# Sharing out the PSUM banks of two attentions anew: two banks for scores, other banks for the outputs of the values

## The chip, the cores and the metric

The kernel runs on one core of a Trainium2 chip. The metric is the device time of one execution in microseconds (us). The core has a matrix engine, TensorE (PE in the profile), which multiplies and transposes, and writes its results into PSUM, a memory of eight banks of 128 partitions by 512 float32 values. VectorE (DVE), ScalarE (ACT) and GpSimd (POOL) do the elementwise work; SyncE (SP) issues the loads. Each engine works through its own list of instructions in order, and an instruction that needs another engine's result waits for a semaphore; whatever is queued behind it waits with it. A PSUM bank can take new results only when the old ones have been read, so a tile that gets a bank waits for the last reader of the tile that had it before.

## The reference

A sequence of 512 tokens with 1024 features goes through two layers, each an attention, an output projection, a layer norm, a SwiGLU FFN and a layer norm.

```
# layer A: differential attention, 8 heads, two score matrices (m) for each
for i in range(s // Q_BLOCK):                       # 4 query tiles of 128
    sc = einsum('bqhmd,bkhmd->bhmqk', q[:, q0:kend], k[:, :kend])
    p = softmax(where(allowed, sc, neg))
    a = p[:, :, 0] - lam * p[:, :, 1]
    outs.append(einsum('bhqk,bkhe->bqhe', a, v[:, :kend]))
o = rms_norm(concatenate(outs), subln_g) * (1.0 - lambda_init);  return o @ w_o
# layer B: band attention, 16 heads, learned bias, one shared K/V
sc = einsum('bnqhd,bnkhd->bhnqk', q, k_band) + bias
p = softmax(where(band_valid, sc, neg))
o = einsum('bhnqk,bnkhd->bnqhd', p, v_band);  return o @ w_o
# both
x = layer_norm(ALPHA * x + mix);  x = layer_norm(ALPHA * x + (silu(gate) * up) @ w_out)
```

All data is float32; the large products are made of three matrix products of parts rounded to a shorter format (`hi`/`lo` of the weights, `xTh`/`xTl` of the activations, `oTh`/`oTl` of the attention's outputs).

## The kernel before, in words

Each layer's attention is cut into 32 units: 8 heads (in layer B pairs of heads) times 4 query tiles; a unit of query tile `qt` has `(qt + 1) * 128` keys. The units run through a software pipeline written out by hand. A step of layer A's pipeline (`STEPS`, line 50) issues on TensorE: the scores `s` of unit i, filling work, the product with the values `o` of unit i-2, the transpose `ot` of unit i-3, more filling work, and the transposes `at` of unit i-1. The filling work is the q, k and v projections of later heads and, at the end, the first matmuls of the output projection. `weave` mixes the two by the rates in `FA` and `FB`, with a model of how long each engine takes; `chain` and `later` put the work of the other engines in their queues when the model says that its inputs are there. So the order of each engine's list follows from the model, and a tile's bank enters into it, because the model knows when the bank's last tile was read.

What one unit of layer A does (`unit_a`): `sc`, two score tiles (m = 0, 1) on TensorE; VectorE adds the mask and takes the row minimum of the negated sum (`masked`, the profile's `e<-sc,mask` and `nm`); ScalarE takes the exponentials with their sum; VectorE mixes the two (`e<-e,c`); TensorE transposes (`at`), ScalarE copies the result (`aT`), TensorE multiplies with the values (`o`); ScalarE squares it for the norm (`sq`), GpSimd makes the root (`ms`, `rr`), VectorE scales (`sq<-o,rr,gsub`); TensorE transposes again (`ot`), ScalarE rounds it into `oTh`, and VectorE takes the rest (`oTl<-ot,oTh`). The q and k projections end in a rotation, on VectorE in part: `krc`, `kla_g`, `ks`, `qs`.

In layer B (`unit_b`, `values_b`) a unit has the scores `sc_b` of two heads, `masked` with the bias, the exponentials, the scaling (`e_b<-e_b,r_b`), and the transposes `pt_b` of each head, which ScalarE (`pth`) and VectorE (`ptl<-pt_b,pth`) read; when a pair's four query tiles are there, `values_b` makes `po` for each of its heads, which ScalarE (`tl`) and VectorE (`ot<-po,tl`) read.

The banks: the pool `psp` has four tags of two banks. `pj` serves the projections. `sc0` and `sc1` serve the scores, one bank of each per unit (`pair`), so two units' scores fit. `sm` serves in layer A `at`, `o` and `ot`, in layer B `pt_b` and `po` of both heads. Within a tag the banks are given in turn. The output projection takes `pj` and a `pair` for the first half of its columns, two pairs for the second.

Of the kernel before, what the change touches and what calls it, by code (L numbers as in the profile page):

```python
# [132 lines left out]
def trunk(ctx, tc, x, a_w_qkv, a_lambda, a_subln_g, a_w_o, kv_w, b_w_q, b_rel_bias, b_w_o,  # L133
# [29 lines left out]
    def new(pool, bufs, shape, dtype, tag, name):  # L163

        old = slots.setdefault((pool.name, tag), [])
        if len(old) >= bufs:
            settle([old[-bufs]])
        t = pool.tile(shape, dtype, tag=tag, name=name)
        if len(old) >= bufs:
            model.replaces(name_of(t), old[-bufs])  # L170
        old.append(name_of(t))
        return t

    def bank(tag, name):
        return new(psp, 2, [P, HALF], F32, tag, name)

    def pair(name):
        return [bank(f"sc{i}", f"{name}_{i}") for i in range(2)]

    def passed(out_, ins, ns, start):  # L180
        at = max([clk[0]] + [model.ready(a) for a in ins] + ([model.unused(out_)] if start else []))
# [270 lines left out]
    def project_out(act, nk, get_xres, banks0, lead, held, gate, ln, tr, name, banks_1=None):  # L452

        begun = banks_1 is not None  # L460

        def step(h, b, t, k, w_, j):
            ts_ = slice(t * P, (t + 1) * P)
            ah, al = act(h, k)
            token_major(b, ah[:, ts_], al[:, ts_], w_[0][:, j, :], w_[1][:, j, :],
                        k == 0 and not begun, k == nk - 1)
            return True

        def add(h, t, b):
            residual(xres[t], b, h, sts[t])  # L470

        b01 = banks0(0)
        ws = []
        for c in range(lead // 2):
            while not gate(2 * c + 1):
                yield True
            ws.append(take(f"{name}_0_{c}"))
            for j in range(2):
                for t in range(2):
                    yield step(0, b01[t], t, 2 * c + j, ws[c], j)  # L480
        while not gate(-1):
            yield True
        b23 = banks0(1)
        for c in range(lead // 2):
            for j in range(2):
                for t in range(2):
                    yield step(0, b23[t], 2 + t, 2 * c + j, ws[c], j)
            free(f"{name}_0_{c}")
        xres = get_xres()
        for c in range(lead // 2, nk // 2):  # L490
            while not gate(2 * c + 1):
                yield True
            w_ = take(f"{name}_0_{c}")
            for j in range(2):
                for t in range(NT):
                    yield step(0, (b01 + b23)[t], t, 2 * c + j, w_, j)
            free(f"{name}_0_{c}")
        sts = []
        for t in range(NT):
            sts.append(small.tile([P, 2, 6], F32, tag="st", name=f"st_{name}_{t}"))  # L500
        for t in (2, 3, 0, 1) if lead else range(NT):
            add(0, t, (b01 + b23)[t])
        banks = banks_1 or pair(f"{name}_1a") + pair(f"{name}_1b")
        split = (nk - held) // 2
        for c in range(split):
            w_ = take(f"{name}_1_{c}")
            for j in range(2):
                for t in range(NT):
                    yield step(1, banks[t], t, 2 * c + j, w_, j)
            free(f"{name}_1_{c}")  # L510
        ws = []
        for t in range(NT):
            for i in range(held // 2):
                if t == 0:
                    ws.append(take(f"{name}_1_{split + i}"))
                for j in range(2):
                    yield step(1, banks[t], t, 2 * (split + i) + j, ws[i], j)
                if t == NT - 1:
                    free(f"{name}_1_{split + i}")
            add(1, t, banks[t])  # L520
            ln(t, xres[t], sts[t])
            if tr and t in (1, 2):
                tr(t - 1, xres[t - 1])
# [519 lines left out]
    def unit_a(h, qt):  # L1043

        kend = (qt + 1) * P
        n_ = f"{h}_{qt}"
        sc = pair(f"sc_{n_}")
        scores(sc, *qk[h], qt)
        e = new(ap3, 3, [P, 2, HALF], F32, "e", f"e_{n_}")
        nm = ap6.tile([P, 2], F32, tag="nm", name=f"nm_{n_}")  # L1050
        s = ap6.tile([P, 2], F32, tag="s", name=f"s_{n_}")
        r = ap6.tile([P, 2], F32, tag="r", name=f"r_{n_}")

        def top():
            masked(sc, (mask, mask), e, nm, kend)

        def ex():
            for m in range(2):
                act_e.activation(e[:, m, :kend], e[:, m, :kend], AF.Exp, scale=-1.0, bias=nm[:, m:m + 1],
                                     accum_out=s[:, m:m + 1])  # L1060

        def mix():
            vec_e.reciprocal(r, s)
            c = ap6.tile([P, 1], F32, tag="c", name=f"c_{n_}")
            vec_e.scalar_tensor_tensor(c, s[:, 0:1], r[:, 1:2], nlam, op0=ALU.mult, op1=ALU.mult)
            vec_e.scalar_tensor_tensor(e[:, 0, :kend], e[:, 1, :kend], c, e[:, 0, :kend],
                                           op0=ALU.mult, op1=ALU.add)

        chain([*sc, e], (lambda: sc, top), (lambda: [nm], ex), (lambda: [s], mix))
        yield e  # L1070
        pt = bank("sm", f"at_{n_}")
        for kt in range(qt + 1):
            transpose(pt[:, kt * P:(kt + 1) * P], e[:, 0, kt * P:(kt + 1) * P])
        aT = new(ap2, 2, [P, HALF], F32, "aT", f"aT_{n_}")
        chain([aT, pt], (lambda: [pt], lambda: act_e.copy(aT[:, :kend], pt[:, :kend])))
        yield aT
        po = bank("sm", f"o_{n_}")
        for kt in range(qt + 1):
            mm(po[:, 0:P], aT[:, kt * P:(kt + 1) * P], vt[kt][:, h * P:(h + 1) * P],
               start=(kt == 0), stop=(kt == qt), cost=4.0)  # L1080
        sq = new(ap2, 2, [P, P], F32, "sq", f"sq_{n_}")
        ms = ap6.tile([P, 1], F32, tag="ms", name=f"ms_{n_}")
        rr = ap6.tile([P, 1], F32, tag="rr", name=f"rr_{n_}")

        def root():
            pool_e.tensor_scalar(ms, ms, 1.0 / P, SUBLN_EPS, op0=ALU.mult, op1=ALU.add)
            pool_e.tensor_tensor(rr, ms, mexp, op=ALU.pow)
            pool_e.tensor_tensor(rr, rr, r[:, 0:1], op=ALU.mult)

        chain([sq, po], (lambda: [po], lambda: act_e.activation(  # L1090
            sq, po[:, 0:P], AF.Square, scale=r[:, 0:1], accum_out=ms)), (lambda: [ms], root), (
            lambda: [rr], lambda: vec_e.scalar_tensor_tensor(sq, po[:, 0:P], rr, gsub, op0=ALU.mult, op1=ALU.mult)))
        yield sq
        pu = bank("sm", f"ot_{n_}")
        transpose(pu[:, 0:P], sq)
        oh = oTh[:, h, qt * P:(qt + 1) * P]
        chain([pu, oTh, oTl], (lambda: [pu[:, 0:P]], lambda: act_e.copy(oh, pu[:, 0:P])), (
            lambda: [oh], lambda: vec_e.tensor_sub(
                oTl[:, h, qt * P:(qt + 1) * P], pu[:, 0:P], oh.bitcast(F32))))
        yield  # L1100
# [38 lines left out]
    def o_proj(oh, ol, res_src, l, name):  # L1139
        def get_xres():  # L1140
            del xres[:]
            for t in range(NT):
                xt = resid.tile([P, D], F32, tag="res", name=f"{name}_x_{t}")
                load_e.dma_start(xt, res_src(t))
                xres.append(xt)
            lng.append(ln_params(l, 0))
            return xres

        def banks0(i):
            if i == 0:  # L1150
                return [bank("pj", f"{name}_0_{j}") for j in range(2)]
            return pair(f"{name}_0_23")

        def gate(k):
            return done["s"] if k < 0 else done["o"] >= k

        yield from project_out(
            lambda h, k: (oh[:, k, :], ol[:, k, :]), KT, get_xres, banks0, 6, 8, gate,
            lambda t, xr, st: spill(layer_norm(xr, st, *lng[-1], f"{l}0_{t}"), x1d[l], t, xr),
            lambda t, xr: transpose_split(xr, t), name)  # L1160
# [123 lines left out]
    def unit_b(p, qt):  # L1284
# [1 line left out]
        bias = biases[p]  # L1286
        kend = (qt + 1) * P
        n_ = f"b{p}_{qt}"
        sc = pair(f"sc_{n_}")
        scores(sc, *qk[p], qt)  # L1290
        e = new(bp2, 2, [P, 2, HALF], F32, "e", f"e_{n_}")
        mx = small.tile([P, 2], F32, tag="nm", name=f"mx_{n_}")
# [17 lines left out]
        yield e  # L1310
        _, pth, ptl = held[p]
        for m in range(2):
            pt = bank("sm", f"pt_{n_}_{m}")
            for kt in range(qt + 1):
                transpose(pt[:, kt * P:(kt + 1) * P], e[:, m, kt * P:(kt + 1) * P])
            dh = pth[m][:, qt * P:qt * P + P]
# [11 lines left out]
    def values_b(p):  # L1328
# [1 line left out]
        ot = new(bp2, 2, [P, S], F32, "ot", f"ot_{p}")  # L1330
        steps, used = [], [ot, oTh, oTl]
        for m in range(2):
            po = bank("sm", f"po_{p}_{m}")
            for kt, lo in ((0, 0), (1, 128), (2, 256), (3, 256)):
                for i, src in enumerate((pth[m], ptl[m])):
                    mm(po[:, lo:S], vs[:, kt, m, :, :].rearrange("p a e -> p (a e)"),
# [100 lines left out]
```

## Time and profile before

| | us |
|---|---|
| median of 3 runs | 1239.59 (1236.62 to 1242.48) |
| the profiled execution, own time | 1239.44 |
| its span | 1237.7 |
| PE busy in the span | 1192.2 (96%) |
| DVE busy | 834.9 (67%) |
| ACT busy | 556.3 (45%) |
| POOL busy | 405.5 (33%) |

The span reaches from the first to the last recorded instruction of the core; the own time of the execution has a little around it. "Busy" counts the time in which an engine computes. The attentions run from about 45 to 240 us (layer A) and from about 660 to 860 us (layer B), each with its projections and followed by output projection and FFN. An engine's wait is put down to the instruction that released it, with the line of that one.

### The profile page before, as it was taken

Reading aid. Unit: us, or ns where it says so; the run is one execution under the profiler, and the core shown is the slowest. Engines: PE = TensorE matmul, PEld = TensorE weight load, DVE = VectorE, ACT = ScalarE, POOL = GpSimd, SP = SyncE. Lnnn points to the kernel's source line nnn. Section 1 sums busy time; section 2 is a strip of 40 time slices with the busy share of each in tenths; the row PEclk is TensorE's granted clock in tenths of the full one; section 3 lists DMA queues with packets and bytes.
Section 4 is the critical chain, followed back from the end, with each engine's and each line's share of the span. In section 5 each row is a group of like instructions: output and inputs, shape, how many; then the busy total and the mean of one; then the engine's idle time right before and its main releaser. Section 6 shows DMA issues by size and latency. Waiting matters only on the chain.

```text
span 1237.7 us, 19979 instructions
## 1 busy us (share of the span) xinstructions
PE 1192.2 (96%) x7640; PEld 1078.5 (87%) x7640; DVE 834.9 (67%) x1451; ACT 556.3 (45%) x1049; POOL 405.5 (33%) x410
## 2 busy tenths in 40 slices
PE   8989989899999999999999999989999999999997
PEld 7867877788999999888887888978899999998886
DVE  4677777388678888533465767675888888883327
ACT  4556666425444444322145667663454444443220
POOL 1134343421555564000323233214136666620022
PEclk9999999899999999999999999999999999999999
DMA  8433342245544443533344342335433333353311
GB/s 265 124 89 95 87 110 86 76 153 145 153 139 138 138 124 104 187 98 124 102 119 116 98 120 65 107 94 170 135 98 108 103 103 103 103 176 114 102 68 69
DMA packets 164191, 145.74 MB, mean 118 GB/s; under 512 B 6096, under 2 KB 137456, under 8 KB 164096
## 3 DMA queue, kind: packets, MB, share of 16 engines
q1 hardware_dynamic: 164096, 144.47, 38.6%
q8 instruction: 60, 0.98, 0.3%
q14 instruction: 35, 0.29, 0.1%
HBM read 127.63 MB, written 13.67 MB: 114 GB/s over the span
## 4 chain that ended last, share of the span: by engine, by line
PE 86%; DVE 7%; ACT 3%; issue 2%; DMA 1%; POOL 1%; SPq 0%; DVEq 0%; ACTq 0%; POOLq 0%
PE m L194 31%; PE c L194 5%; PE a L194 5%; PE b L194 5%; PE gu L194 5%; PE d L194 4%; PE vb_ps L194 4%; PE bk_ps L194 3%; PE bq_ps L194 3%; PE va_ps L194 3%; PE q_ps L194 2%; PE k_ps L194 2%; PE sc_b L194 2%; PE po L194 2%; PE pt_b L199 2%
## 5 line engine op out<-in xcount | busy, mean ns | idle before, releaser
L75 ACT ACTIVATE sg<-sg 128x512 f32<-128x512 f32 x38 | 24.1, 633 | 194.8 <-DVE sg L75 194.8
L75 POOL TENSOR_TENSOR sums<-raw_u 128x512 f32<-128x512 f32 x38 | 49.0, 1291 | 190.6 <-DVE s3lo L75 173.3
L75 POOL TENSOR_TENSOR lo_fo<-raw_fo,hi_fo 128x1024 fp32r<-128x1024 f32 x8 | 19.2, 2394 | 217.2 <-ACT hi_fo L75 217.2
L75 DVE TENSOR_TENSOR lo_fk<-raw_fk,hi_fk 128x1024 fp32r<-128x1024 f32 x28 | 33.9, 1223 | 66.4 <-ACT hi_fk L75 66.4
L75 POOL TENSOR_TENSOR sums<-raw_g,sums 128x512 f32<-128x512 f32 x38 | 76.6, 2016 | 0.0
L75 DVE TENSOR_TENSOR m<-m,m 128x256 f32<-128x256 f32 x76 | 31.7, 417 | 62.8 <-PE m L194 62.8
L75 ACT CAST hi_fk<-raw_fk 128x1024 fp32r<-128x1024 f32 x28 | 29.4, 1052 | 76.0 <-PE d L194 70.9
L75 DVE TENSOR_TENSOR alo<-raw_g,ahi 128x1024 fp32r<-128x1024 f32 x38 | 55.0, 1447 | 0.0
L75 POOL TENSOR_TENSOR sums<-sums,raw_g 128x512 f32<-128x512 f32 x38 | 49.8, 1311 | 3.9 <-DMA raw_g<-in_ffn_w_in_dram 1.1
L75 POOL TENSOR_TENSOR sums<-raw_g,raw_u 128x512 f32<-128x512 f32 x38 | 50.1, 1319 | 0.0
L75 DVE TENSOR_TENSOR s1lo<-sums,s1hi 128x1024 fp32r<-128x1024 f32 x38 | 46.0, 1211 | 0.0
L75 DVE TENSOR_TENSOR s3lo<-sums,s3hi 128x1024 fp32r<-128x1024 f32 x38 | 46.0, 1211 | 0.0
L75 ACT CAST hi_fo<-raw_fo 128x1024 fp32r<-128x1024 f32 x16 | 16.9, 1055 | 64.5 <-PE d L194 64.5
L194 PE MATMUL m<-T1h,s1hi 128*128 128x256 f32 x152 | 43.0, 283 | 0.0
L194 PE MATMUL m<-T1l,s1hi 128*128 128x256 f32 x152 | 43.0, 283 | 0.0
L194 PE MATMUL m<-T1h,s1lo 128*128 128x256 f32 x152 | 43.0, 283 | 0.0
L194 PE MATMUL m<-T2g,s1hi 128*128 128x256 f32 x152 | 43.0, 283 | 0.0
L194 PE MATMUL m<-T2b,s1hi 128*128 128x256 f32 x152 | 43.0, 283 | 0.0
L194 PE MATMUL m<-T2g,s1lo 128*128 128x256 f32 x152 | 43.0, 283 | 0.0
L194 PE MATMUL m<-T3h,s3hi 128*128 128x256 f32 x152 | 43.0, 283 | 0.0
L194 PE MATMUL m<-T3l,s3hi 128*128 128x256 f32 x152 | 43.0, 283 | 0.0
L194 PE MATMUL m<-T3h,s3lo 128*128 128x256 f32 x152 | 43.0, 283 | 0.0
(612 smaller groups left out, 4761.6 us busy)
## 6 DMA issues: line engine op xcount, KB each, us to landing
raw_g<-in_ffn_w_in_dram SPq DMA_DIRECT2D x44, 512.0 KB, 3.9
raw_u<-in_ffn_w_in_dram SPq DMA_DIRECT2D x44, 512.0 KB, 5.1
raw_fk<-in_ffn_w_out_dram SPq DMA_DIRECT2D x28, 512.0 KB, 3.6
raw_fo<-in_ffn_w_out_dram SPq DMA_DIRECT2D x16, 512.0 KB, 3.7
skew<-extd SPq DMA_DIRECT2D x16, 320.0 KB, 6.0
raw_va<-in_a_w_qkv_dram SPq DMA_DIRECT2D x8, 512.0 KB, 4.2
raw_q<-in_a_w_qkv_dram SPq DMA_DIRECT2D x8, 512.0 KB, 5.1
raw_k<-in_a_w_qkv_dram SPq DMA_DIRECT2D x8, 512.0 KB, 4.1
```

The lines of the kernel that those rows point to most:

```text
L75: return issue(*args, **kwargs)
L194: nc.tensor.matmul(out_, lhsT, rhs, start=start, stop=stop)
L199: nc.tensor.transpose(out_, in_, ident)
```

## The change

In both attentions a unit's two score tiles now take the two banks of `sc0` (`twice("sc0", ...)`), where they took one of `sc0` and one of `sc1`. In layer A, `o` takes `sc1`, where it took `sm`; `at` and `ot` stay in `sm`. In layer B the transposes and the outputs of the first head of a pair stay in `sm`, those of the second take `sc1`. The output projection follows: both `sc0` banks for two of its four accumulators of the first half, `sc1` twice and `sc0` twice for the second half. The number of instructions on each engine is the same.

```diff
--- before.py
+++ after.py
@@ -177,6 +177,9 @@
     def pair(name):
         return [bank(f"sc{i}", f"{name}_{i}") for i in range(2)]
 
+    def twice(tag, name):
+        return [bank(tag, f"{name}_{i}") for i in range(2)]
+
     def passed(out_, ins, ns, start):
         at = max([clk[0]] + [model.ready(a) for a in ins] + ([model.unused(out_)] if start else []))
         clk[0] = at + ns
@@ -500,7 +503,7 @@
             sts.append(small.tile([P, 2, 6], F32, tag="st", name=f"st_{name}_{t}"))
         for t in (2, 3, 0, 1) if lead else range(NT):
             add(0, t, (b01 + b23)[t])
-        banks = banks_1 or pair(f"{name}_1a") + pair(f"{name}_1b")
+        banks = banks_1 or twice("sc1", f"{name}_1a") + twice("sc0", f"{name}_1b")
         split = (nk - held) // 2
         for c in range(split):
             w_ = take(f"{name}_1_{c}")
@@ -1044,7 +1047,7 @@
 
         kend = (qt + 1) * P
         n_ = f"{h}_{qt}"
-        sc = pair(f"sc_{n_}")
+        sc = twice("sc0", f"sc_{n_}")
         scores(sc, *qk[h], qt)
         e = new(ap3, 3, [P, 2, HALF], F32, "e", f"e_{n_}")
         nm = ap6.tile([P, 2], F32, tag="nm", name=f"nm_{n_}")
@@ -1074,7 +1077,7 @@
         aT = new(ap2, 2, [P, HALF], F32, "aT", f"aT_{n_}")
         chain([aT, pt], (lambda: [pt], lambda: act_e.copy(aT[:, :kend], pt[:, :kend])))
         yield aT
-        po = bank("sm", f"o_{n_}")
+        po = bank("sc1", f"o_{n_}")
         for kt in range(qt + 1):
             mm(po[:, 0:P], aT[:, kt * P:(kt + 1) * P], vt[kt][:, h * P:(h + 1) * P],
                start=(kt == 0), stop=(kt == qt), cost=4.0)
@@ -1147,9 +1150,7 @@
             return xres
 
         def banks0(i):
-            if i == 0:
-                return [bank("pj", f"{name}_0_{j}") for j in range(2)]
-            return pair(f"{name}_0_23")
+            return twice("sc0" if i else "pj", f"{name}_0_{i}")
 
         def gate(k):
             return done["s"] if k < 0 else done["o"] >= k
@@ -1286,7 +1287,7 @@
         bias = biases[p]
         kend = (qt + 1) * P
         n_ = f"b{p}_{qt}"
-        sc = pair(f"sc_{n_}")
+        sc = twice("sc0", f"sc_{n_}")
         scores(sc, *qk[p], qt)
         e = new(bp2, 2, [P, 2, HALF], F32, "e", f"e_{n_}")
         mx = small.tile([P, 2], F32, tag="nm", name=f"mx_{n_}")
@@ -1310,7 +1311,7 @@
         yield e
         _, pth, ptl = held[p]
         for m in range(2):
-            pt = bank("sm", f"pt_{n_}_{m}")
+            pt = bank(("sm", "sc1")[m], f"pt_{n_}_{m}")
             for kt in range(qt + 1):
                 transpose(pt[:, kt * P:(kt + 1) * P], e[:, m, kt * P:(kt + 1) * P])
             dh = pth[m][:, qt * P:qt * P + P]
@@ -1330,7 +1331,7 @@
         ot = new(bp2, 2, [P, S], F32, "ot", f"ot_{p}")
         steps, used = [], [ot, oTh, oTl]
         for m in range(2):
-            po = bank("sm", f"po_{p}_{m}")
+            po = bank(("sm", "sc1")[m], f"po_{p}_{m}")
             for kt, lo in ((0, 0), (1, 128), (2, 256), (3, 256)):
                 for i, src in enumerate((pth[m], ptl[m])):
                     mm(po[:, lo:S], vs[:, kt, m, :, :].rearrange("p a e -> p (a e)"),
```

TensorE's list in layer A, at the second head's first units. The names are those above with head's query tile and a serial number; in brackets stands which engine's semaphore an instruction waits for. Before:

```order
L199 MATMUL ot_2_950<-ident,sq_2_887 128x128 [waits PE_49]
L199 MATMUL at_0_963<-ident,e_0_875 128x128 [waits DVE_49]
L194 MATMUL sc_2_0_966<-ks_787,qs_714 128x384
L194 MATMUL sc_2_0_966<-kla_b,qs_714 128x384
L194 MATMUL sc_2_1_967<-ks_787,qs_714 128x384
L194 MATMUL sc_2_1_967<-kla_b,qs_714 128x384
L194 MATMUL o_0_977<-va_323,aT_0_965 128x128 [waits DVE_49,Activation_49]
L199 MATMUL ot_3_984<-ident,sq_3_947 128x128
```

and now:

```order
L202 MATMUL ot_2_942<-ident,sq_2_887 128x128 [waits DVE_49]
L197 MATMUL q_ps_852<-xTh_a,hi_q_708 128x512
L197 MATMUL q_ps_852<-xTl_a,hi_q_708 128x512
L197 MATMUL q_ps_852<-xTh_a,lo_q_710 128x512
L202 MATMUL at_0_953<-ident,e_0_875 128x128 [waits DVE_49,PE_49]
L197 MATMUL sc_2_0_966<-ks_787,qs_714 128x384 [waits DVE_49]
L197 MATMUL sc_2_0_966<-kla_b,qs_714 128x384
L197 MATMUL sc_2_1_967<-ks_787,qs_714 128x384 [waits DVE_49]
L197 MATMUL sc_2_1_967<-kla_b,qs_714 128x384
L197 MATMUL o_0_976<-va_323,aT_0_955 128x128 [waits Activation_49]
```

Three matmuls of a projection have come between `ot` and `at`; the first score matmul of each tile waits for VectorE, and `o` waits for ScalarE alone.

VectorE's list at the same place (`e_0` is the mix of unit 0 of the head, the four ISA rows are the masked reductions of unit 1). Before:

```order
L75 SCALAR_TENSOR_TENSOR e_0_875<-e_0_875,c_0_909 128x128
L75 TENSOR_TENSOR krc_848<-krc_848,ksw_843 128x512
L75 ISA e_1_925,nm_1_926<-sc_1_0_918,mask 128x256
L75 ISA nm_1_926 128x1
L75 ISA e_1_925,nm_1_926<-sc_1_1_919,mask 128x256
L75 ISA nm_1_926 128x1
L75 TENSOR_TENSOR kla_g<-krc_848,ks_913 64x512 x2
```

and now:

```order
L75 SCALAR_TENSOR_TENSOR e_0_875<-e_0_875,c_0_914 128x128
L75 ISA e_1_923,nm_1_924<-sc_1_0_917,mask 128x256
L75 ISA nm_1_924 128x1
L75 ISA e_1_923,nm_1_924<-sc_1_1_918,mask 128x256
L75 ISA nm_1_924 128x1
L75 TENSOR_TENSOR krc_848<-krc_848,ksw_843 128x512
L75 TENSOR_TENSOR oTl<-ot_2_942,oTh 128x128
```

The masked reductions have moved ahead of the krc addition, and `oTl` of the unit before follows it directly.

TensorE's list in layer B, at the second pair of heads, before:

```order
L199 MATMUL pt_b_0_0_7380<-ident,e_b_0_7260 128x128 [waits DVE_49]
L199 MATMUL pt_b_0_1_7382<-ident,e_b_0_7260 128x128 [waits DVE_49]
L194 MATMUL sc_b_2_0_7385<-bks_7016,bqs_6980 128x384
L194 MATMUL sc_b_2_0_7385<-klb_b,bqs_6980 128x384
L194 MATMUL sc_b_2_1_7386<-bks_7016,bqs_6980 128x384
L194 MATMUL sc_b_2_1_7386<-klb_b,bqs_6980 128x384
L194 MATMUL vb_ps_1_7224<-hi_vb_0_7021,xTh_b 128x256
```

and now:

```order
L202 MATMUL pt_b_0_0_7377<-ident,e_b_0_7260 128x128 [waits DVE_49,PE_49]
L202 MATMUL pt_b_0_1_7379<-ident,e_b_0_7260 128x128 [waits DVE_49,PE_49]
L197 MATMUL sc_b_2_0_7382<-bks_7016,bqs_6980 128x384 [waits DVE_49]
L197 MATMUL sc_b_2_0_7382<-klb_b,bqs_6980 128x384
L197 MATMUL sc_b_2_1_7383<-bks_7016,bqs_6980 128x384 [waits DVE_49]
L197 MATMUL sc_b_2_1_7383<-klb_b,bqs_6980 128x384
L197 MATMUL vb_ps_1_7224<-hi_vb_0_7021,xTh_b 128x256
```

The order of the matmuls is the same; the first matmul of each score tile now waits for VectorE.

## Rows read from the trace of the kernel before

**Rows 1.** Busy time by stretch: start:end, length, each engine's busy time, clock, DMA.

```profile
45.00:230.00 185.00, 166.45 (x938) 140.64 (x937) 134.96 (x348) 111.42 (x313) 63.06 (x105) 0.97 0.32 88
670.00:900.00 230.00, 219.95 (x1302) 192.78 (x1302) 164.95 (x395) 132.96 (x322) 65.49 (x95) 0.99 0.35 108
```

**Rows 2.** TensorE's waits, layer A's attention: us in total, times, longest.

```profile
PE at L199 <- DVE oTl L75: 12.5, 12, 3.7
...
PE at L199 <- DVE sq L75: 0.3, 1, 0.3
```

**Rows 3.** Timeline, TensorE: start, us of one, instruction, wait ahead.

```profile
77.79 0.33 PE L199 MATMUL at<-ident,e 128*128 128x128 f32 x1 [1.37 <-DVE oTl L75]
...
80.33 0.27 PE L199 MATMUL ot<-ident,sq 128*128 128x128 f32 x1
84.30 0.33 PE L199 MATMUL at<-ident,e 128*128 128x128 f32 x1 [3.70 <-DVE oTl L75]
```

**Rows 4.** Timeline of VectorE over the same wait.

```profile
79.98 0.69 DVE L75 TENSOR_TENSOR krc<-krc,ksw 128x512 f32<-128x512 f32 x1
80.58 0.42 DVE L75 CUSTOM_DVE_ANT_0 e<-sc,mask 128x256 f32<-128x256 f32 x1
...
83.96 0.28 DVE L75 TENSOR_TENSOR oTl<-ot,oTh 128x128 fp32r<-128x128 f32 x1
```

**Rows 5.** TensorE's waits, layer B's attention.

```profile
PE pt_b L199 <- DVE ot L75: 3.2, 5, 1.0
PE ob L194 <- DVE klb_b L75: 2.1, 1, 2.1
PE pt_b L199 <- DVE e_b L75: 1.6, 1, 1.6
PE pt_b L199 <- DVE ptl L75: 0.9, 2, 0.7
```

**Rows 6.** Timeline of TensorE around 120 us.

```profile
119.79 0.55 PE L199 MATMUL at<-ident,e 128*128 128x128 f32 x3 [1.91 <-DVE oTl L75]
...
122.42 0.39 PE L194 MATMUL o<-va,aT 128*128 128x128 f32 x2
```

**Rows 7.** Timeline of ScalarE at the same place.

```profile
121.44 0.49 ACT L75 COPY aT<-at 128x384 f32<-128x384 f32 x1
```

**Rows 8.** Timeline of TensorE at the end of layer A's units.

```profile
217.70 0.36 PE L194 MATMUL sc<-ks,qs 128*128 128x256 f32 x1 [1.79 <-DMA ks<-ks]
...
227.66 0.27 PE L199 MATMUL ot<-ident,sq 128*128 128x128 f32 x1
228.92 0.69 PE L199 MATMUL at<-ident,e 128*128 128x128 f32 x2 [0.98 <-DVE oTl L75]
229.26 0.78 PE L194 MATMUL sc<-ks,qs 128*128 128x512 f32 x1
```

**Rows 9.** Timeline of VectorE at the same place.

```profile
226.87 0.35 DVE L75 SCALAR_TENSOR_TENSOR sq<-o,rr,gsub 128x128 f32<-128x128 f32 x1 [0.74 <-POOL rr L75]
227.14 0.55 DVE L75 CUSTOM_DVE_ANT_0 e<-sc,mask 128x384 f32<-128x384 f32 x1
```

**Rows 10.** Busy time by stretch, columns as in rows 1: two stretches at half clock.

```profile
85.54:88.96 3.42, 3.42 (x12) 2.74 (x11) 2.07 (x9) 1.81 (x7) 0.93 (x3) 0.50 0.00 0
218.66:225.49 6.83, 5.78 (x26) 4.80 (x24) 3.41 (x14) 3.46 (x14) 0.93 (x3) 0.50 0.00 0
```

**Rows 11.** Timelines of VectorE and TensorE at the start of layer B.

```profile
669.67 0.42 DVE L75 CUSTOM_DVE_ANT_0 e_b<-sc_b,bias 128x256 f32<-128x256 f32 x1 [1.71 <-PE sc_b L194]
...
669.85 0.42 PE L194 MATMUL sc_b<-bks,bqs 128*128 128x384 f32 x1
```

**Rows 12.** Timelines of VectorE and TensorE, layer A's second half of the output projection.

```profile
266.53 0.69 DVE L75 SCALAR_TENSOR_TENSOR oa_x<-oa_x,oa_1b 128x512 f32<-128x512 f32 x1 [0.64 <-PE oa_1b L194]
...
272.65 0.28 PE L194 MATMUL gu<-xTh_a,hi_g 128*128 128x256 f32 x1
```

**Rows 13.** Busy time of a stretch of layer A, columns as in rows 1.

```profile
115.00:125.00 10.00, 8.09 (x66) 7.69 (x64) 9.65 (x25) 7.42 (x20) 1.46 (x6) 1.00 0.27 79
```

## The prediction

> **What bounds the kernel now.** I read the busy time by stretch first. In both attention stretches the fullest engine is TensorE, with holes: 166.45 of 185 us in layer A, 219.95 of 230 in layer B, while VectorE, the next in line, has 134.96 and 164.95 [rows 1]. So the time of an attention is TensorE's work plus its waits, and a change that leaves the matmuls as they are can touch only the waits and the clock.
>
> The table of waits says which. In layer A, 12.5 us in 12 waits are `at <- DVE oTl`, and 0.3 is `at <- DVE sq` [rows 2]. That is a wait for a bank, not for data: `sm` has two banks, and `at`, `o` and `ot` rotate through them, so the transposes of a unit go into the bank that the `ot` just ahead of them was written to, and stand until VectorE has read it. The costliest shows it: `ot` starts at 80.33, and `at`, next in the queue, at 84.30 after a wait of 3.70 us [rows 3], though its own operand was written by the VectorE instruction ahead of the krc addition that starts at 79.98. VectorE then did that addition, two masked reductions, `kla_g` and another mix, and `oTl<-ot,oTh` ran from 83.96 to 84.24 [rows 4]. In layer B the waits of this kind are `pt_b <- DVE ot` 3.2 and `<- DVE ptl` 0.9, together 4.1; those on `klb_b` (2.1) and `e_b` (1.6) are for data [rows 5].
>
> The profiled execution took 1239.44 us, its span 1237.7 and 1.7 around it; the median of the three runs is 1239.59. I sum against 1239.44 and leave the 1.7 as it is.
>
> **Part 1, layer A: `o` moves to `sc1`.** Then `at` and `ot` alternate in `sm`, each with a bank of its own. An `at` waits for the copy `aT<-at` of the unit before, which the `o` of that unit has waited for already, and an `ot` for the `oTl` one unit earlier. All 12.8 us of bank waits can go. They don't all stay gone, because VectorE and ScalarE come little earlier, and TensorE arrives sooner at the next thing it needs from them:
> - 76 to 85 us, waits of 1.37 and 3.70 [rows 3]: behind them the scores of the next unit now need the masked reductions, which start at 80.58, after the krc addition [rows 4]. The new order puts them ahead of it, so both end near 79.98 + 2 x 0.42 = 80.8, about when TensorE arrives. I give back 0.5.
> - The wait of 1.91 ahead of 119.79: the `o` that follows at 122.42 [rows 6] needs `aT`, which a busy ScalarE had at 121.44 + 0.49 = 121.93 [rows 7]. TensorE can be 0.49 sooner there, and a little more where the copy is due earlier. I give back 1.2.
> - The tail, three waits of 0.88 to 0.98 (the last of them in [rows 8]), 2.74 in all: the `ot` at 227.66 needs `sq`, ready at 226.87 + 0.35 = 227.22 [rows 9], so at most 0.44 passes there. Back: 0.8.
> - The rest, 12.8 - 1.37 - 3.70 - 1.91 - 2.74 = 3.1, in waits of under 1 us. One of 0.3 runs into the wait of 1.79 for the DMA of `ks` at 217.70 [rows 8]; of the others I let 0.5 pass on. Back: 0.8.
> Sum: 12.8 - 0.5 - 1.2 - 0.8 - 0.8 = **9.5** gained.
>
> **Part 2, the clock.** Four stretches ran at a granted 0.50, that is 1.2 of 2.4 GHz: one of 3.42 us of busy time at 85.54, right after the 3.70 wait, one of 5.78 at 218.66, after the 1.79 wait for `ks` [rows 10], and two more like the first, at 228.90 among the tail's waits and at 822.82 after the `klb_b` wait. The engine had stood ahead of each. At half clock matmuls take up to twice as long, so a stretch that returns gives at most half of its busy time: 1.7, 2.9, 1.7 and 1.7. The first loses its cause, the second and the fourth keep theirs, the third loses part of it. I take 1.7 + 0.6 = **2.3**; the bounds are 0 and 1.7 + 2.9 + 1.7 = 6.3.
>
> **Part 3, scores in one pair.** A unit's two score tiles now take both `sc0` banks, so its scores wait for the previous unit's masked reductions; before, for those of the unit before that. No trace of before shows this wait, so I bound it by the distance from the end of a reduction to the next scores' start. In layer A the smallest of 31 is 229.26 - (227.14 + 0.55) = 1.57 us [rows 8, 9]: nothing, with TensorE up to 1.5 us earlier against VectorE. In layer B 13 of 31 are under 3 us, and the smallest is 669.85 - (669.67 + 0.42) = -0.24 [rows 11]. Only that one and the next are below zero, and they stand around the `e_b` wait of 1.6 us [rows 5], which swallows the first; the second costs **0.3**. If every reduction came 3 us later against TensorE, the sum over the units would be 18.1 in B and 3.2 in A. I take the near end, since a reduction hangs on earlier scores and moves with them.
>
> Of the rules for this, the Trainium skill speaks against this part: "Perfetto Trace Analysis", section "Optimizing Tensor Performance", Matmuls, wants independent groups to rotate through different PSUM banks, so that reading out one overlaps the next group's matmuls. By it the far end, 21.3, would hold. The trace agrees only for the two transitions below zero; elsewhere the reading is over before the next group starts.
>
> **Part 4, layer B: a transpose bank for each head.** `pt_b` and `po` of head 0 stay in `sm`, those of head 1 go to `sc1`, so a tile finds its bank free unless the one two before it is still unread. Of the 4.1 us [rows 5] I count all, less the 0.3 of part 3: **3.8**.
>
> **Edits at nothing.** An output projection takes both `sc0` banks for the first output half of two token tiles, free once the last unit's masked reductions are done, and `o` of that unit needs those anyway. In its second half `sc1` and `sc0` change places, so SwiGLU's first gate matmuls, at 272.65, find another tile's bank; VectorE read that one into its residual by 266.53 + 0.69 = 267.22 [rows 12], 5.4 us earlier. With this cover gone it would cost the read, 0.7. The planner also moves ScalarE's exponentials behind a copy, and some rows on GpSimd and SyncE within the attentions; ScalarE and GpSimd are under 61% busy there [rows 1], and the loads keep their order. Matmuls, and the FFN with its order, are the same.
>
> **Sum:** 9.5 + 2.3 + 3.8 = 15.6; 1239.44 - 15.6 = 1223.8, about **1224**.
>
> **Rivals.**
> *The waits only pass on.* From 115 to 125 us VectorE is busy 9.65 of 10 us [rows 13]. If it is the bound there, and also where it held the waits of 1.37 and 3.70 and about 1.3 of the small ones, these 8.3 us give nothing; of the tail's 2.7 only 0.9 is won, of B's 3.8 half, and no clock: 12.8 - 8.3 - 1.8 + 1.9 = 4.6, time **1235**. For it: that row. Against it: rows 4, where `oTl` stood behind work that TensorE didn't need next.
>
> *Slower: the shared score pair.* If the reductions fall 3 us behind TensorE once the bank waits no longer hold it back, part 3 costs 18.1 + 3.2 = 21.3 in new waits against 15.6 won: **1245**. It decides from about 2.7 us of lag on. For it: VectorE's load in rows 13, and that a wait at the scores holds every matmul queued behind them. Against it: the 1.57 of rows 8 and 9, and that the lag I can show in part 1 is 0.5.
>
> *Everything goes, and the clock comes back.* All 12.8 less 0.4, all 4.1, and 6.3 of clock: 22.8, time **1217**. For it: nothing that `at` reads was late in any of its waits. Against it: the `ks` wait is left, and so its half-clock stretch.
>
> That the tiles keep their old banks is excluded: the order shows `sc` waiting on VectorE now, and `o` no longer.
>
> **How the numbers follow.** Forecast (1218 to 1231) 0.62; waits pass on 0.16; all goes and the clock returns 0.15; slower 0.07. The range 1216 to 1235 takes in the forecast, the third rival and the near half of the first, and leaves out the slower one and the first one's far half, about 0.15. A measurement of this kernel can tell some 0.5% from no change, 6.2 us. The forecast and the third rival lie beyond that; of the first rival most (0.13) lies within and the rest (0.03) beyond: faster 0.62 + 0.15 + 0.03 = 0.80, same 0.13, slower 0.07.
>
> **What would show it.** In the trace of after: no `at <- DVE oTl` row and no `pt_b <- DVE ot`; `sc <- DVE` rows of under 1 us in A and about 0.3 in B; rows `o <- ACT aT` and `ot <- DVE sq` grown by some 3 us together; no half-clock stretch near 85; layer B shorter by about 4 us, layer A by about 12. Rows of `sc_b <- DVE` of many microseconds, or attentions as long as before with the waits under other names, would make it wrong.

## The result, and the profile after

The changed kernel is faster: 1226.71 us median (1223.74 to 1227.07, 4 runs) against 1238.11 (1236.05 to 1242.48, 4 runs), a ratio of 0.990 with an interval of 0.987 to 0.993. Measured a second time, beside the experiments below, it had 1224.09 against 1239.75, ratio 0.986 (0.984 to 0.987). The forecast was 1224, a gain of 15.6; the medians moved by 11.4 and by 15.7. The profiled execution took 1223.74 us with a span of 1222.0, so the two profiles lie 15.7 apart, and that is what the views below divide up.

Busy time by stretch, cut at the same matmuls before and after: layer A's attention, layer B's, the FFN between them with what belongs to it, the start, the rest (another 25.9 us, the second half of layer A's output projection, lie between layer A's attention and the FFN in both). The columns are start:end, length, busy time of PE, PE's weight loads, DVE, ACT and POOL with the number of instructions, granted clock, DMA share, GB/s. Of before:

```profile
55.43:249.56 194.13, 175.57 (x978) 147.82 (x978) 134.78 (x345) 113.55 (x318) 72.96 (x117) 0.96 0.33 95
661.55:858.77 197.22, 189.14 (x1100) 164.97 (x1099) 132.22 (x349) 123.24 (x310) 57.65 (x94) 0.99 0.33 103
275.45:661.55 386.10, 382.55 (x2628) 356.39 (x2627) 252.13 (x328) 148.29 (x192) 126.51 (x91) 1.00 0.44 132
0.00:55.43 55.43, 50.13 (x322) 46.04 (x322) 27.45 (x48) 24.34 (x44) 6.01 (x15) 1.00 0.70 203
858.77:1237.70 378.93, 369.26 (x2489) 341.75 (x2487) 265.24 (x346) 138.66 (x176) 137.01 (x89) 0.99 0.35 108
```

and of after, with the FFN ahead of layer B:

```profile
56.94:240.84 183.90, 172.34 (x978) 147.59 (x978) 135.17 (x344) 112.46 (x318) 72.26 (x117) 0.97 0.35 99
266.79:651.30 384.51, 380.95 (x2628) 354.93 (x2627) 258.10 (x328) 149.25 (x192) 138.53 (x91) 1.00 0.44 132
651.30:843.08 191.78, 187.37 (x1101) 164.95 (x1100) 131.42 (x350) 122.44 (x310) 57.26 (x94) 0.99 0.34 105
0.00:56.94 56.94, 51.60 (x322) 47.31 (x323) 27.46 (x48) 24.42 (x44) 6.00 (x15) 1.00 0.68 198
843.08:1222.00 378.92, 369.25 (x2489) 341.79 (x2487) 265.89 (x346) 138.52 (x176) 136.03 (x90) 1.00 0.36 109
```

Layer A's attention is 10.2 us shorter. Its idle time (length less PE's busy time) fell from 18.6 to 11.6, by 7.0; PE's busy time fell by 3.2 with as many matmuls. Layer B's is 5.4 shorter: 3.7 of idle time and 1.8 of busy time. The start is 1.5 us longer and the FFN stretch 1.6 shorter, with nothing changed in either; in both it is PE's busy time alone that differs, with the same number of matmuls. This is the clock. In the FFN stretch the kernel before ran at half clock (0.50) behind a wait of 1.61 us for `hb`:

```profile
283.52:286.93 3.41, 3.41 (x18) 3.41 (x17) 2.17 (x4) 3.12 (x6) 1.01 (x1) 0.50 1.17 294
```

The changed kernel has the same wait and no such stretch. At the start the views list 1.00 for both, but the matmuls show the same: four of `va_ps<-lo_va,xTh_a` started 0.12 us apart at 10.59 in before and 0.21 apart at 10.77 in after, where the pace of before came only at 13.3. In the half-clock stretch above matmuls of this size start 0.21 apart, too. That the two cancel is chance. The rest is the same to 0.01.

TensorE's waits after (us in total, times, longest), in layer A:

```profile
PE o L197 <- ACT aT L75: 6.1, 4, 2.9
PE sc L197 <- DMA ks<-ks: 2.4, 2, 2.3
PE ot L202 <- DVE sq L75: 1.2, 1, 1.2
PE oa L197 <- DVE nm L75: 1.2, 1, 1.2
PE at L202 <- DVE e L75: 0.4, 1, 0.4
```

and in layer B:

```profile
PE ob L197 <- DVE klb_b L75: 3.1, 1, 3.1
PE pt_b L202 <- DVE e_b L75: 1.2, 1, 1.2
```

Beside [rows 2, 5]: the bank waits, 12.8 us of `at` and 4.1 of `pt_b`, are gone altogether. What has come up in layer A is an `o` waiting for `aT`, an `ot` for `sq`, and `oa`, the output projection, for `nm`, a masked reduction.

### The profile page after: what moved, and what is told of

Its sections match the earlier page's. It is cut to its first block, busy times and chain, and to the rows that moved or that the text cites. A ratio compares the mean times of both kernels' runs of the same rounds, so it can differ in the third digit from the quotient of the medians.

```text
span 1222.0 us, 19996 instructions
## 1 busy us (share of the span) xinstructions
PE 1187.1 (97%) x7640; PEld 1078.1 (88%) x7640; DVE 841.6 (69%) x1451; ACT 555.3 (45%) x1049; POOL 415.5 (34%) x410
## 4 chain that ended last, share of the span: by engine, by line
PE 86%; DVE 6%; ACT 3%; issue 2%; POOL 1%; DMA 1%; SPq 0%; DVEq 0%; ACTq 0%; POOLq 0%
PE m L197 31%; PE c L197 5%; PE a L197 5%; PE b L197 5%; PE gu L197 5%; PE d L197 4%; PE vb_ps L197 4%; PE bq_ps L197 3%; PE bk_ps L197 3%; PE va_ps L197 3%; PE k_ps L197 3%; PE q_ps L197 3%; PE ob L197 2%; PE po L197 2%; PE sc_b L197 2%
## 5 line engine op out<-in xcount | busy, mean ns | idle before, releaser
L75 POOL TENSOR_TENSOR sums<-raw_g,sums 128x512 f32<-128x512 f32 x38 | 86.4, 2274 | 0.0
L75 DVE TENSOR_TENSOR alo<-raw_g,ahi 128x1024 fp32r<-128x1024 f32 x38 | 50.2, 1322 | 0.1
L75 ACT CAST s3hi<-sums 128x1024 fp32r<-128x1024 f32 x38 | 40.0, 1052 | 6.9 <-POOL sums L75 3.6
```

Source lines behind the costliest of these rows:

```text
L75: return issue(*args, **kwargs)
```

## The experiments

**The change once more (e0), layer A alone (e1), layer B alone (e2), the shared scores alone (e3).** The edits, each on the kernel that it names:

```diff
# e1: the changed kernel, with layer B's lines as before
-        sc = twice("sc0", f"sc_{n_}")                    # in unit_b
+        sc = pair(f"sc_{n_}")
-            pt = bank(("sm", "sc1")[m], f"pt_{n_}_{m}")
+            pt = bank("sm", f"pt_{n_}_{m}")
-            po = bank(("sm", "sc1")[m], f"po_{p}_{m}")
+            po = bank("sm", f"po_{p}_{m}")
# and in o_proj and project_out the banks of before where name == "ob"
# e2: the kernel before, with those lines of layer B as in the change
# e3: the kernel before, with this alone, in unit_a and in unit_b
-        sc = pair(f"sc_{n_}")
+        sc = twice("sc0", f"sc_{n_}")
```

> The changed kernel once more, beside the parts. Theory (the bank waits went, the shared scores cost nothing): about 1226, ratio to before 0.988 to 0.992. The profile pair differed by 15.7 us but the medians by 11.4; if the difference is made by half-clock stretches that fall differently from run to run (about 1.7 us each), this profile shows another number of such stretches than the first one, and its matched stretches of layer A and layer B are again about 10 and 5 us shorter than before's.

> Layer A's banks as in the change, layer B's as before. Theory (each attention gains by its own bank waits): layer A's stretch about 10 us shorter than before, layer B's as before, with its five pt_b waits on ot (3.2 us) back; time about 7 to 10 under before, ratio near 0.993. Rival (layer A's waits only pass on, and the gain is the clock's or layer B's): less than 4 us.

> Layer B's banks as in the change, layer A's as before. Theory: layer B's stretch about 5 us shorter, layer A's unchanged with its 12 waits of at on oTl; time about 4 to 5 under before, ratio near 0.996; with the other part's gain it adds up to the whole change's, within 2 us. Rival (the shared scores cost in layer B, where 13 of 31 distances are under 3 us): no gain, and rows sc_b waiting on VectorE.

> Only the scores share one pair of banks in both layers; o, pt_b and po stay in sm, so two banks stand idle during the attentions. Theory (the scores' second pair was not used: reductions are over before the next scores start): time of before within 2 us, the at waits on oTl as before (12.5 us), rows sc waiting on VectorE of under 1 us in all. Rival (sharing has a price that the change's gain hides): slower by 3 us or more, with sc or sc_b rows waiting on VectorE.

Measured, against 1239.75 of before on the same chip:

| | median us | ratio | interval | mean clock of the runs |
|---|---|---|---|---|
| e0, the change | 1224.09 | 0.986 | 0.984 to 0.987 | 0.992 to 0.994 |
| e1, layer A alone | 1229.00 | 0.990 | 0.988 to 0.991 | 0.992 to 0.996 |
| e2, layer B alone | 1235.77 | 0.995 | 0.994 to 0.997 | 0.985 to 0.993 |
| e3, shared scores alone | 1242.62 | 1.0015 | 1.0004 to 1.0027 | 0.987 to 0.993 |

The parts add up: by the ratios 1.0% and 0.5% against 1.4%. In e0's trace layer A's stretch is 9.1 us and layer B's 5.3 us shorter than before, as expected, with 13.7 us at half clock in layer A where the first trace of the change has 10.2. In e1's trace layer A's stretch is 10.2 us shorter (by the starts of the same matmuls) and layer B's has its old waits; in e2's trace it is the other way round, with layer B 5.6 shorter and these waits of `at` in layer A:

```profile
PE at L202 <- DVE oTl L75: 13.5, 13, 3.7
```

So the first rival, that layer A's waits only pass on, falls. e3 has the old waits in both layers and none for the reductions; these are its rows for layer A:

```profile
PE at L202 <- DVE oTl L75: 13.5, 12, 3.7
PE o L197 <- ACT aT L75: 3.4, 3, 2.6
PE sc L197 <- DMA ks<-ks: 1.9, 2, 1.8
PE at L202 <- DVE sq L75: 0.3, 1, 0.3
```

and for layer B:

```profile
PE pt_b L202 <- DVE ot L75: 3.2, 5, 1.0
PE ob L197 <- DVE klb_b L75: 2.1, 1, 2.1
PE pt_b L202 <- DVE e_b L75: 1.2, 1, 1.2
PE pt_b L202 <- DVE ptl L75: 0.9, 2, 0.7
```

Yet it measured 0.15% slower, 1.9 us by its ratio and 2.9 by the medians, between the 2 that was expected and the 3 of its rival. Most of this goes with the clock: its five runs at a mean granted clock of 0.988 average 1242.1, and eight runs of before at the same clock 1241.5; at 0.987 it is 1242.8 and 1242.2, five runs each. At equal clock 0.6 is left; part 3 below finds 0.3 of it in e3's trace. Why e3's runs fell to the lower clock more often isn't settled, so whether that is a price of the shared scores stays open.

The clocks of the runs also go with the difference between the 11.4 and the 15.7 that the change measured. Within one kernel the runs line up by clock, over all measurements: before has 1242.2 on average at 0.987, 1239.9 at 0.990 (8 runs) and 1237.86 at 0.992 (3 runs), some 0.9 us for each 0.001. Three of the change's first four runs stood at 0.990, with 1226.8; of the later ones two stood at 0.992, with 1224.24. At equal clock the change is worth 13.1 and 13.6.

**ScalarE's order (e5).** In the changed kernel's trace, the `o` of the longest wait, and ScalarE's timeline ahead of it (start, us, instruction, idle time before it and who ended it):

```profile
105.16 0.49 PE L197 MATMUL o<-va,aT 128*128 128x128 f32 x2 [2.94 <-ACT aT L75]
```

```profile
101.41 0.24 ACT L75 CAST oTh<-ot 128x128 fp32r<-128x128 f32 x1
103.56 1.26 ACT L75 CAST ks<-krc 64x512 fp32r<-64x512 f32 x2 [1.90 <-DVE krc L75]
104.84 0.27 ACT L75 COPY aT<-at 128x128 f32<-128x128 f32 x1
```

The copy `aT` took 0.27 us, and its transposes had started at 100.55. ScalarE stood for 1.90 us before it, because the cast of the keys, next in its queue, needed VectorE's krc addition. The wait of 2.65 at 157.5 has the same order behind it. There the krc addition itself was long, too:

```profile
155.77 2.68 DVE L75 TENSOR_TENSOR krc<-krc,ksw 128x512 f32<-128x512 f32 x1
155.27 2.63 POOL L75 TENSOR_TENSOR lo_va<-raw_va,hi_va 128x1024 fp32r<-128x1024 f32 x1 [0.28 <-ACT hi_va L75]
```

Of the kernel's 16 krc instructions on VectorE 14 take 0.68 or 0.69 us. The other two, this one and one of 2.41 at 95.43, are the only ones that start while a `lo_va` of GpSimd runs, and both end 0.55 us after it. No run tests what holds the addition back. The edit lets the planner queue the cast 2 us later:

```diff
-                chain([rc, st], (lambda: [rc], high), (lambda: [st], last))
+                def split():
+                    chain([rc, st], (lambda: [rc], high), (lambda: [st], last))
+                if nm == "k" and 1 < h < 7:
+                    later(2000.0, split, rc, st)
+                else:
+                    split()
```

> The changed kernel, with ScalarE's rounding cast of the keys (ks<-krc) put into its queue 2 us later by the planner for the heads 2 to 6, which puts it behind the copy aT that it stood ahead of at the two places where the changed kernel's o waits for aT (2.94 at 102 us and 2.65 at 158 us). Theory (what was given back in layer A is ScalarE's order: the cast waits for VectorE's krc addition, and aT, whose transposes were long done, queues behind it): both waits go, and with them the half-clock stretches that begin right after them (105.55 and 160.16, 3.41 us each, worth 1.7 each), so 5.6 + 3.4 = 9.0 us less, of which I expect 1 to 2 to come up elsewhere: 1216 to 1219 where the changed kernel again has 1224 to 1227. Rival (aT is late because ScalarE and VectorE are full, whatever their order): the waits stay under the same or another name, less than 2 us gained.

Measured: 1217.40 median, ratio 0.982 (0.980 to 0.984), as the theory had it. The long addition of 2.68 is still in its trace (at 150.51); the copy no longer stands behind it. The two waits are gone, with 1.5 us of `o <- ACT aT` left, and the half-clock stretches that began right behind them have gone too. In the changed kernel they are

```profile
105.55:108.96 3.41, 3.41 (x10) 2.75 (x9) 1.92 (x7) 1.60 (x5) 2.22 (x1) 0.50 0.32 75
160.16:163.58 3.42, 3.39 (x11) 2.90 (x12) 3.29 (x9) 2.02 (x7) 0.74 (x2) 0.50 0.79 206
```

and in e5's trace the granted clock is 1.00 from 12.8 to 214.2 us. The timeline of its ScalarE at that place has the copy first and the cast of the keys fourth:

```profile
100.79 0.27 ACT L75 COPY aT<-at 128x128 f32<-128x128 f32 x1 [0.91 <-PE at L202]
100.95 0.59 ACT L75 COPY qr<-q_ps 128x512 f32<-128x512 f32 x1
101.43 1.06 ACT L75 CAST hi_va<-raw_va 128x1024 fp32r<-128x1024 f32 x1
102.38 1.26 ACT L75 CAST ks<-krc 64x512 fp32r<-64x512 f32 x2
```

**The output projection's banks (e6, and e7 with the later cast).** The two waits at the end of layer A's units, in the changed kernel's timeline of TensorE:

```profile
219.13 0.33 PE L202 MATMUL ot<-ident,sq 128*128 128x128 f32 x1 [1.24 <-DVE sq L75]
...
221.79 0.79 PE L197 MATMUL oa<-hi_oa,oTh 128*128 128x512 f32 x1 [1.19 <-DVE nm L75]
```

The second is the edit that I had put at nothing. The output projection takes both `sc0` banks right behind the last unit's scores, in the queue ahead of that step's `o`, `ot` and `at`, and so waits for the reductions of scores that have just been made. The edit opens that half of it a step later:

```diff
             rates = FA[0] if i < FA[2] else FA[1] if i < nu else FA[3]
+            done["s"] = i >= nu
...
-                    done["s"] = i == nu - 1
```

> The changed kernel, with the output projection of layer A kept out of the sc0 banks for one step more, so that o, ot and at of the last units are issued ahead of its first matmul there. Theory (the wait oa <- DVE nm of 1.2 us is the price of the edit that was costed at nothing: those banks are free only after the last unit's masked reductions): this wait goes or falls under 0.3, time 0.5 to 1.2 less than the changed kernel. Rival (the end of the units is bound by VectorE's chain): the 1.2 come back as a wait of o, ot or at there, no difference.

> The later cast (1217.4 by itself) and the output projection kept out of sc0 for one step (whose wait of 1.2 us went) together. Theory: the two waits are at different places and both stay gone: about 1216, 1 us under the later cast alone, with no row oa <- DVE nm and o <- ACT aT under 2 us. Rival (with the cast's time won, VectorE's chain ends the units): 1217 to 1218, no difference.

Measured: e6 1222.93, ratio 0.986 (0.984 to 0.987), where the change had 0.986; e7 1217.72, 0.982 (0.981 to 0.984), where e5 had 0.982. The wait on `nm` is gone in both, and neither ratio differs from that of the kernel it was added to. In e7 `ot <- DVE sq` has grown from e5's 1.4 us in 2 waits to

```profile
PE ot L202 <- DVE sq L75: 2.6, 3, 1.3
```

so there its rival holds: the wait came back under another name. In e6 that row stays at 1.2, and TensorE's idle time in layer A is 1.2 less, as the theory had it. Its trace shows layer A 2.6 us shorter, with one half-clock stretch less there and one of twice the length in layer B, and the runs don't tell the 1.2 from nothing.

**The wait on `klb_b` (e8, e9, e10).** I had called it a wait for data. It is another bank wait: the output projection of layer B starts in `pj`, whose last tile is the key projection of the last heads, which `klb_b` reads. The change let TensorE arrive earlier, and it grew from 2.1 to 3.1. The edit of e8, on the changed kernel, makes the last values the last filling work:

```diff
-    FILL_B = [..., ("qk", 6), ("v", 3), ("qk", 7)]
+    FILL_B = [..., ("qk", 6), ("qk", 7), ("v", 3)]
```

e9 is this on e5. e10 is this on e7, with the output projection of layer B, too, opened a step later (the edit of e6, in `attention_b`).

> The changed kernel, with the last two pieces of layer B's filling work swapped: the projections of the last pair of heads before the last values. Theory (the wait ob <- DVE klb_b, 2.1 us before and 3.1 after the change, is a bank wait too, on pj, whose last tile is the key projection that klb_b reads; the change made it longer by letting TensorE arrive earlier): it goes, and with it the half-clock stretch that follows it (808.70, 3.41 us, 1.7): 4.8 us less than the changed kernel. Rival (the data of the output projection is late): the wait stays under another name, no difference.

> The edits of the later cast and of the swapped filling work together. Theory: they are in different layers and add up: 9.0 + 4.8 less 1 to 2, about 1212 where the changed kernel has 1224 to 1227. Rival: what one gives the other doesn't, above 1217.

> As the run with the later cast and the later output projection, and in layer B the swapped filling work with its output projection kept out of sc0 for one step more, too. Swapping alone turned the wait on klb_b of 3.1 us into one on the masked reductions of 2.3 and several small ones. Theory (those are bank waits of the sc0 pair, which the later start avoids): both go, 3 us of waits and a half-clock stretch (1.7) less than without the swap, about 1212. Rival (layer B then has too little filling work left at its end, and TensorE waits for the units themselves, as pt_b <- DVE e_b): 1216 or more.

Measured: e8 1224.66, 0.988 (0.986 to 0.990); e9 1219.22, 0.983 (0.981 to 0.985); e10 1215.80, 0.9805 (0.979 to 0.982). Swapping gained nothing, neither alone nor on e5, as the rivals of e8 and e9 had it. The wait on `klb_b` went, but the output projection then met another one, for the `sc0` pair:

```profile
PE ob L197 <- DVE mx_b L75: 2.3, 1, 2.3
PE pt_b L202 <- DVE e_b L75: 1.2, 1, 1.2
```

With the later start (e10) that one goes as well, and a wait for data of 1.4 comes up:

```profile
PE pt_b L202 <- DVE e_b L75: 2.6, 2, 1.4
PE sc_b L197 <- DVE mx_b L75: 0.4, 1, 0.4
...
PE pt_b L202 <- DVE ot L75: 0.3, 1, 0.3
```

e10 is 3.8 us short of what was expected of it, 0.2 from its rival, which had named this wait on `e_b`. It is the fastest version that ran, 24 us under the kernel before. Its five runs lie within 0.3 us of each other (1215.62 to 1215.93) at mean clocks of 0.995 to 0.997, where the nine of before beside them spread over 4.9: in its trace no wait of layer B is followed by half clock any more.

## Why the prediction was right, point by point

**What bounds the kernel, and what the waits are:** right. The waits of `at` and `pt_b` were for banks, all went, and each part alone gave its share (e1, e2). The planner also made new lists from the new banks, and no run has the new banks with the old lists, so what the order adds by itself isn't shown.

**Part 1, 9.5 us for layer A.** The idle time fell by 7.0. What failed is the giving back: I had 3.3 and it was 5.8 (12.8 less 7.0), and the places were others than I named. Ahead of 120 us, where I gave back 1.2, an `o` waits 0.13. The 2.94 at 102 I didn't see, because ScalarE's queue was read only where a wait of before stood; e5 shows that ScalarE's order makes the wait; why VectorE's addition came so late isn't tested. The tail gave back 1.24 where I had 0.8, the DMA of `ks` 0.5 where I had 0.3.

**Part 2, 2.3 us of clock.** In layer A's stretch the half-clock stretches hold 10.0 us of busy time after (the two above and 3.2 at 221.6) against 12.6 before, 1.3 gained in this pair of profiles. The first one went, as forecast; but the 2.94 and the 2.65 wait each brought one, the latter wait being about as long before (2.55 at 164.93) without one. I had counted four half-clock stretches in before and overlooked the fifth, the one at 283.52: its 1.6 us are in no term, and only the later rise of the clock at the start, 1.5 us, hides that in the pair of profiles. Over the runs the mean clock rose from 0.9895 to 0.991 in the first measurement and to 0.993 in the second, which at 0.9 us for 0.001 is 1.2 to 3: the size was right, and it is the part that varies from run to run.

**Part 3, 0.3 us for the shared scores.** The two places where I had found the distance below zero are the ones in layer B where the reductions just hold the scores up. The first of them, VectorE's reduction and the scores behind it:

```profile
659.42 0.42 DVE L75 CUSTOM_DVE_ANT_0 e_b<-sc_b,bias 128x256 f32<-128x256 f32 x1 [1.71 <-PE sc_b L197]
```

```profile
659.91 0.45 PE L197 MATMUL sc_b<-bks,bqs 128*128 128x384 f32 x1
```

The scores start 0.07 us after the reduction's end at 659.84. TensorE shows less than 0.1 of idle time there, but idle time is not the whole price, because matmuls overlap in the records. From a transpose's start to that of the score behind it it is 0.03 us at 35 places of after; here it is 0.34, and 0.31 at the second place, 663.05. Between the two the `e_b` wait is 0.3 shorter than before (1.2 against 1.6). So the first hold is swallowed and the second costs 0.3, as forecast; e3's trace has the same.

In layer A I had counted nothing. There, too, the scores are held up at two places, 81.34 and 84.24, by some 0.2 us each. The first, with VectorE's reduction ahead of it:

```profile
80.86 0.42 DVE L75 CUSTOM_DVE_ANT_0 e<-sc,mask 128x256 f32<-128x256 f32 x1
```

```profile
81.09 0.30 PE L202 MATMUL at<-ident,e 128*128 128x128 f32 x1 [0.36 <-DVE e L75]
81.34 0.45 PE L197 MATMUL sc<-ks,qs 128*128 128x384 f32 x1
```

The smallest distance from a reduction to the next scores was 1.57 us before and is 0.06 now, and 16 of 31 are under 3 us, where 6 were. "Moves with them" was wrong for layer A: with the bank waits gone TensorE gained on VectorE. e3 can't show this, because it keeps those waits. In all some 0.7 us against 0.3 forecast, and far from the 21.3 of the slower rival. The Trainium skill wants independent groups to rotate through different PSUM banks ("Perfetto Trace Analysis", section "Optimizing Tensor Performance", Matmuls). The trace agrees at these four of the 62 transitions; at the other 58 the reduction was over 0.3 us or more before.

**Part 4, 3.8 us for layer B.** The idle time fell by 3.7: 4.1 and 0.6 of two other waits (`e_b` from 1.6 to 1.2, `oTl` 0.2) went, and the grown wait on `klb_b` took 1.0 back. Calling that wait one for data was a wrong reading. That 3.8 and 3.7 agree so closely is luck: neither the 0.6 nor the 1.0 was in the sum. The stretch gave 5.4 all the same, by the next point.

**Edits at nothing.** The output projection's `sc0` pair was not: 1.2 us of wait in layer A. That the last reductions are "needed anyway" is true of `o` of that unit, but the projection stands ahead of it in the queue. The exchange of banks in the second half did cost nothing: 25.9 us before and after.

**What no term had:** 1.8 us of busy time in layer B, and 1.9 of layer A's 3.2 (3.2 less 1.3 of clock). See the last section.

**The sum.** 13.3 without the clock was forecast, and 13.1 and 13.6 measured at equal clock: too little given back and the missing term about cancel. So the waits were read rightly, and that the sum is so close is luck. The rival in which everything goes and the clock returns was wrong for this kernel, but it is near what e5 reached, 1217.4.

## What to carry to other kernels

A wait on a reader of another tile is a wait for a bank; share banks so that a tile doesn't follow, in its bank, the one that was written just ahead of it in the queue, and a second buffer that no wait needs may pay for this. Its margin shrinks, though, when the waits go: here from 1.57 us to 0.06. When such waits go, look along every engine's queue for an instruction that waits ahead of a short one which TensorE needs next: here a cast in front of a copy cost nearly half of what was given back. Before a bank change is put at nothing, find the first writer of each bank in the queue, not in the data flow.

## What the runs showed of the hardware that I had not expected

A wait costs more than its idle time. In layer B both profiles have one half-clock stretch of 3.41 us, and yet PE's busy time is 1.8 us less with the eight waits on `ot`, `ptl` and `oTl` (4.3 us) gone, some 0.2 us a wait even with the two holds of part 3 in it. The traces of e0, e2 and e5 agree, with 1.7 to 1.9 less than before. Some 1.2 of it are the transposes, which had waited, shown here before and after, by form (busy time, mean ns of one, idle time ahead and who ended it):

```profile
L199 PE MATMUL at<-ident,e 128*128 128x128 f32 x80 | 15.8, 298 | 13.1 <-DVE oTl L75 12.5 <-DVE sq L75 0.3
...
L199 PE MATMUL pt_b<-ident,e_b 128*128 128x128 f32 x160 | 25.1, 284 | 5.8 <-DVE ot L75 3.2 <-DVE e_b L75 1.6 <-DVE ptl L75 0.9
```

```profile
L202 PE MATMUL at<-ident,e 128*128 128x128 f32 x80 | 14.3, 278 | 0.4 <-DVE e L75 0.4
...
L202 PE MATMUL pt_b<-ident,e_b 128*128 128x128 f32 x160 | 23.9, 280 | 1.3 <-DVE e_b L75 1.2
```

One reading, not tested: matmuls in a row overlap, as an `sc` that starts at 100.58 in after, 0.03 us behind the start of an `at` that takes 0.27; the first one behind a wait has none to overlap with.

And the clock isn't fixed by the kernel: the same instructions in the same order ran layer A with 12.6 us of half-clock busy time in the trace of before and with 19.6 in e2's, where layer A is the same:

```profile
84.29:91.12 6.83, 5.36 (x17) 4.67 (x18) 4.11 (x14) 2.81 (x13) 1.98 (x6) 0.50 0.14 30
220.82:237.89 17.07, 14.19 (x51) 12.06 (x52) 8.55 (x32) 7.73 (x30) 3.53 (x11) 0.50 0.01 3
```

Layer A took 3.3 us longer in that trace. Runs of the kernel before beside e0 lie up to 6.2 us apart, at mean clocks of 0.987 to 0.991; what decides the clock in a run isn't settled.
